# Decay rows by a broadcast DMA instead of matmuls, and parts of the gates and of head 4 in another order

## The chip, the cores and the metric

One core of a Trainium2 chip runs the whole program. The metric is the device time of one execution in microseconds (us). One more execution was taken with a profile; its rows are what is read here.

## What is computed

Two transformer blocks on a sequence of 512 positions with 1024 features, in fp32. The first (stick-breaking attention and a gated FFN) is not touched. The second projects its input, runs two mixers, joins them through two gates, and ends in an MLP. The change lies in the first mixer, branch A, a gated delta rule with 8 heads of 128 query and key features and 256 value features:

```python
qkv = jax.nn.silu(causal_depthwise_conv(jnp.concatenate([qa, ka, va], axis=-1), conv_a))
...
g = -jnp.exp(a_log) * jax.nn.softplus(a_dt + dt_bias)
...
g_cum = jnp.cumsum(g, axis=-1)
decay = jnp.exp(jnp.where(causal, g_cum[..., :, None] - g_cum[..., None, :], -jnp.inf))
lower = jnp.where(strict, jnp.einsum('bhncd,bhnmd->bhncm', k_beta, k) * decay, 0.0)
t_inv = lax.linalg.triangular_solve(lower, eye, left_side=True, lower=True, unit_diagonal=True)
...
attn = jnp.where(causal, jnp.einsum('bhncd,bhnmd->bhncm', q, k) * decay, 0.0)
q_exp = q * jnp.exp(g_cum)[..., None]
def step(state, inp):
    qe, ww, uu, aqk, kd, ld = inp
    v_new = uu - jnp.einsum('bhck,bhkv->bhcv', ww, state)
    o = jnp.einsum('bhck,bhkv->bhcv', qe, state) + jnp.einsum('bhcm,bhmv->bhcv', aqk, v_new)
    state = state * ld[..., None, None] + jnp.einsum('bhck,bhcv->bhkv', kd, v_new)
```

## The kernel before, in words

Every large product is fp32 split in two: a weight half of 128 columns is loaded (`raw`), ScalarE casts it to a high part (`wh`, L122 or L125), VectorE subtracts to get the low part (`wl`, L126), and TensorE does three matmuls for each of 8 slices of the contraction: a unit of 24 matmuls for 128 output features, in one PSUM bank of 512 columns (`psa`, `psg` or `pso`; there are 4, 2 and 2 of them). Two `raw` buffers and four pairs `wh`, `wl` run ahead of TensorE. The loads are issued by SyncE, in the order of the program. All other tiles of branch A live in 32 equal slots (`s`), which go round in the order in which they come free.

Branch A works with chunks of 128 positions, four of them (NT), and two groups of four heads, g0 (heads 0 to 3) and g1 (4 to 7). For each head: `qk_proj` (projection, convolution of 4 taps by L1042 on VectorE, silu by L1046 on ScalarE), `prepare` (norms, scores, decays), and for a group at once `solve` (31 pairs of small steps on VectorE, L1195 and L1198, each waiting for the one before) and `delta_inverse` (joins the blocks that `solve` inverted; its products are masked on POOL by L1225). Then `values_a` (two units, each followed by convolution and silu), `gates_a`, and `delta_scan` (the recurrence over 4 chunks). Projections with no tie to a head (`gate`, `branch_a`) stand between.

`mixer2` writes the order of the large products; the small work is generators that `beside` queues: `yield N` puts the rest of a generator behind N ns of counted TensorE work, `poll` resumes those that are due between matmuls, `until` and `drain` force them. A scheduler then fixes the order of each engine's instructions, and an engine runs them strictly in that order.

The decays: `gates_and_decays` makes g, its sums within a chunk `gc`, and small factors (`ngc` is the negative sum, `kd`, `egl`). `decay_rows` needs for each head the row exp(g_cum) spread over all 128 partitions (`er`), and the masked decay matrix (`dc`, in the program `decT`). Before, TensorE spreads them: four fp32 matmuls of a broadcast g with the triangle `cum` into one bank (`psa<-cst,g`), an exp on ScalarE (L1019) for `er`, four bf16 matmuls that add the mask (`psa<-mb,identb`), and four exps with a bias (L1028) for `dc`.

Of the kernel before, what the change touches and what calls it, by code (L numbers as in the profile page):

```python
# [9 lines left out]
F32 = mybir.dt.float32  # L10
# [60 lines left out]
class Net:  # L71
# [360 lines left out]
    def setup(self):  # L432
# [22 lines left out]
        self.ones = self.const("ones", [P, P])  # L455
        nc.vector.memset(self.ones, 1.0)
# [4 lines left out]
        nc.vector.tensor_scalar(tri[:, 1, :], self.ones, -1.0, None, op0=ALU.mult)  # L461
        nc.vector.tensor_copy(tri[:, 2, :], self.ones)
        self.tri, self.mones, self.pones = tri[:, 0, :], tri[:, 1, :], tri[:, 2, :]
        mb = self.const("mb", [P, 2, P], BF16)

        nc.vector.tensor_scalar(mb[:, 0, :], self.cum, -NEG, NEG, op0=ALU.mult, op1=ALU.add)
        nc.vector.tensor_scalar(mb[:, 1, :], sgn[:, 1, :], NEG, None, op0=ALU.mult)
        self.mask_c, self.mask_s = mb[:, 0, :], mb[:, 1, :]
# [476 lines left out]
    def gates_and_decays(self, acc, heads):  # L945
# [41 lines left out]
        yield 7000  # L987
# [15 lines left out]
        yield from self.decay_rows(heads)  # L1003

    def decay_rows(self, heads):

        nc, S_ = self.nc, self.S
        self.decays = -1
        for h0 in range(heads[0], heads[-1], 2):
            er, dc = self.erow[h0 // 2], self.decT[h0 // 2] = S_.get([P, 2, S]), S_.get([P, 2, S])  # L1010
            ps = []
            for i in range(2):
                p = self.ps("a")
                ps.append(p)
                for n in range(NT):
                    c = slice(n * P, (n + 1) * P)
                    self.mm(p[:, c], self.g[:, n, h0 + i:h0 + i + 1].broadcast_to([P, P]), self.cum,
                            start=(n == 0), stop=False, skip_group_check=True)
                nc.scalar.activation(er[:, i, :], p, AF.Exp)  # L1019
                yield 0  # L1020
            yield 1500
            for i in range(2):
                for n in range(NT):
                    c = slice(n * P, (n + 1) * P)
                    self.mm(ps[i][:, c], self.identb, self.mask_c, start=False, stop=True, skip_group_check=True)
                for n in range(NT):
                    c = slice(n * P, (n + 1) * P)
                    self.last_exp = nc.scalar.activation(dc[:, i, c], ps[i][:, c], AF.Exp,  # L1028
                                                         bias=self.ngc[:, n, h0 + i:h0 + i + 1])
            yield 800  # L1030
# [17 lines left out]
    def first_proj(self, heads):  # L1048

        w = self.a["w_in_2"][0]  # L1050
        r = self.raw(w, 0, KD, O_BE, 16)
# [47 lines left out]
    def prepare(self, h):  # L1099
# [5 lines left out]
        yield 3500  # L1105
# [7 lines left out]
        yield 1600  # L1113
# [421 lines left out]
    def mixer2(self):  # L1535
# [13 lines left out]
        for h in (2, 3):  # L1549
            self.qk_proj(h)  # L1550
# [125 lines left out]
```

## Time and profile before

| what | value |
|---|---|
| median of 3 runs | 2145.35 us (2144.69 to 2147.83) |
| the profiled execution's own time | 2145.01 us |
| its span, first to last instruction | 2142.9 us |
| TensorE (PE) busy | 2079.4 us, 97% |
| VectorE (DVE) busy | 1134.6 us, 53% |
| ScalarE (ACT) busy | 837.8 us, 39% |
| mean granted TensorE clock | 0.994 |
| 680 to 1345 us, branch A up to its last scan: PE busy | 646.9 of 665.0 us |

The profile tells for each engine when it worked and what ended each of its waits. TensorE is busy nearly all the time, so a row matters either when it is TensorE's own work or when TensorE waits for it. Matmuls overlap at their ends: their price is taken from one start to the next, not from the duration of one.

### The profile page before, as it was taken

What the parts mean: (1) busy time and instruction counts of PE and PEld (TensorE: products, weight loads), DVE (VectorE), ACT (ScalarE), POOL (GpSimd) and SP (SyncE); (2) the same over time, 40 slices, a digit from 0 to 9 for tenths busy, and PEclk for the clock granted to TensorE, in tenths of its full rate; (3) what the DMA queues carried; (4) which work ended last, traced back from release to release, by engine and by line L of the source; (5) the groups of instructions that cost most, each with busy time, mean ns of one, the idle gap of its engine ahead of it and who ended that gap; (6) DMA issues with size and microseconds to landing.
All of it is one profiled execution on the core that took longest, in us unless ns stands there. A gap on an engine that the chain in (4) does not pass through costs nothing.

```text
span 2142.9 us, 26115 instructions
## 1 busy us (share of the span) xinstructions
PE 2079.4 (97%) x10498; PEld 1757.2 (82%) x10498; DVE 1134.6 (53%) x1771; ACT 837.8 (39%) x1368; POOL 172.1 (8%) x203
## 2 busy tenths in 40 slices
PE   6899999999999899999998999999999999999998
PEld 5788878888888788888888887888888889888887
DVE  6679778333322565655756545444535475423434
ACT  3587674223212463334522432233232334322422
POOL 2000001000000133000330000010101000000000
PEclk9999999999999999999999999999999999999999
DMA  8715445323232234211342233232222363223322
GB/s 265 211 50 158 142 129 169 117 89 118 89 127 96 103 101 150 78 51 40 125 137 69 83 125 123 84 99 87 77 101 79 139 205 109 98 98 128 98 89 79
DMA packets 172568, 241.93 MB, mean 113 GB/s; under 512 B 13936, under 2 KB 120490, under 8 KB 172448
## 3 DMA queue, kind: packets, MB, share of 16 engines
q1 hardware_dynamic: 168972, 232.65, 33.2%
q0 software_dynamic: 3232, 7.34, 1.5%
q8 instruction: 82, 1.34, 0.3%
q14 instruction: 38, 0.31, 0.0%
q10 hardware_dynamic: 244, 0.29, 0.0%
HBM read 216.59 MB, written 19.41 MB: 110 GB/s over the span
## 4 chain that ended last, share of the span: by engine, by line
PE 84%; DVE 8%; DMA 3%; ACT 2%; issue 1%; POOL 1%; SPq 0%; DVEq 0%; POOLq 0%; ACTq 0%
PE psg L135 37%; PE psa L135 36%; PE pso L135 9%; DMA cv<-ada_w 2%; DVE wl L126 1%; DVE s L1198 1%; PE psa L139 1%; DVE s L1195 1%; DMA s<-ada_w 1%; DVE s L270 1%; DVE s L429 0%; DVE s L501 0%; ACT wh L122 0%; DVE cv L1042 0%; ACT s L291 0%
## 5 line engine op out<-in xcount | busy, mean ns | idle before, releaser
L135 PE MATMUL psg<-s,wh 128*128 128x512 f32 x2368 | 753.5, 398 | 2.5 <-DVE s L1521 2.0
L126 DVE TENSOR_TENSOR wl<-raw,wh 128x1024 fp32r<-128x1024 f32 x306 | 380.9, 1247 | 490.6 <-ACT wh L122 268.8
L135 PEld LDWEIGHTS psg<-s,wh 128*128 128x128 f32 x2368 | 441.1, 189 | 90.7 <-DVE s L1521 2.9
L135 PE MATMUL psa<-wh,s 128*128 128x512 f32 x1536 | 479.1, 391 | 0.3 <-ACT s L272 0.3
L135 PE MATMUL psg<-s,wl 128*128 128x512 f32 x1184 | 464.5, 392 | 0.0
L122 ACT CAST wh<-raw 128x1024 fp32r<-128x1024 f32 x202 | 212.0, 1052 | 436.9 <-PE psg L135 173.7
L135 PEld LDWEIGHTS psa<-wh,s 128*128 128x128 f32 x1536 | 289.4, 189 | 60.3 <-ACT s L272 0.7
L135 PE MATMUL psa<-wl,s 128*128 128x512 f32 x768 | 299.5, 390 | 0.3 <-DVE wl L126 0.3
L135 PEld LDWEIGHTS psg<-s,wl 128*128 128x128 f32 x1184 | 223.2, 189 | 46.7
L135 PE MATMUL psa<-s,s 128*128 128x512 f32 (+3 forms) x760 | 177.4, 364 | 1.0 <-DMA s<-sol 0.6
L135 PEld LDWEIGHTS psa<-wl,s 128*128 128x128 f32 x768 | 144.6, 188 | 30.5 <-DVE wl L126 0.6
L125 ACT CAST wh<-raw 128x1024 fp32r<-128x1024 f32 x104 | 109.1, 1050 | 153.8 <-PE psg L135 122.4
L135 PEld LDWEIGHTS psa<-s,s 128*128 128x128 f32 x760 | 131.1, 190 | 27.4 <-ACT s L1318 2.3
L135 PE MATMUL psg<-wh,s 128*128 128x256 f32 (+1 forms) x672 | 140.9, 298 | 11.0 <-ACT cv L1039 9.2
L135 PE MATMUL pso<-s,wh 128*128 128x512 f32 x448 | 137.9, 389 | 0.0
L135 PEld LDWEIGHTS psg<-wh,s 128*128 128x128 f32 x672 | 110.2, 193 | 16.9 <-ACT cv L1039 9.6
L135 PEld LDWEIGHTS pso<-s,wh 128*128 128x128 f32 x448 | 84.1, 188 | 17.5
L135 PE MATMUL psg<-wl,s 128*128 128x256 f32 (+1 forms) x336 | 97.6, 291 | 0.0
L135 PE MATMUL pso<-s,wl 128*128 128x512 f32 x224 | 87.1, 389 | 0.0
L269 ACT CAST s<-t 128x512 fp32r<-128x512 f32 (+1 forms) x94 | 54.6, 593 | 74.1 <-DVE t L1590 40.6
L270 DVE TENSOR_TENSOR s<-t,s 128x512 fp32r<-128x512 f32 (+1 forms) x94 | 69.2, 747 | 21.3 <-ACT s L269 19.9
L135 PE MATMUL psa<-s,wh 128*128 128x256 f32 x384 | 70.9, 285 | 5.8 <-ACT wh L122 3.1
(244 smaller groups left out, 2199.9 us busy)
## 6 DMA issues: line engine op xcount, KB each, us to landing
raw<-w_in SPq DMA_DIRECT2D x56, 1024.0 KB, 5.2
raw<-ffn_w_in SPq DMA_DIRECT2D x22, 1024.0 KB, 5.1
cv<-ada_w SPq DMA_DIRECT2D x64, 256.0 KB, 4.4
raw<-w_up SPq DMA_DIRECT2D x16, 1024.0 KB, 7.7
raw<-w_down SPq DMA_DIRECT2D x16, 1024.0 KB, 5.1
raw<-sb_w_qkv SPq DMA_DIRECT2D x10, 1024.0 KB
raw<-ffn_w_out SPq DMA_DIRECT2D x10, 1024.0 KB, 6.9
s<-ada_w SPq DMA_DIRECT2D x32, 256.0 KB, 7.3
```

Source lines behind the costliest of these rows:

```text
L122: nc.scalar.copy(h, src)
L125: nc.scalar.copy(h, src)
L126: nc.vector.tensor_sub(l, src, h.bitcast(F32))
L135: self.last_mm = self.nc.tensor.matmul(acc, lhsT, rhs, **kw)
L139: self.last_mm = self.nc.tensor.transpose(out, x, ident)
L269: nc.scalar.copy(dst_h, src)
L270: nc.vector.tensor_sub(dst_l, src, dst_h.bitcast(F32))
L1195: nc.vector.tensor_mul(share, T[:, i, 0:w_].rearrange("p (o j) -> p o j", o=1).broadcast_to([nb, n, w_]), Lb[:, i, i + 1:32].rearrange("p ...
L1198: nc.vector.tensor_add(below, below, share)
```

## The change

Seven edits, all in branch A or in the constants for it.

1. `decay_rows`: the matmuls are gone. `gc` is transposed once for all heads (one PE transpose, one copy on VectorE), written to DRAM (`gcD`, 16 KB), and each head's row is read back by a DMA with a zero step over the 128 partitions (256 KB, pieces of 512 B). VectorE adds bias and mask (four `scalar_tensor_tensor` of 128 x 128 for each head, L1022 of the changed file), ScalarE does two exps of 128 x 512. The function runs at once and no longer as a generator.
2. The constants `mask_c`, `mask_s`, `ones` and `tri` are made a little differently.
3. The delays of `gates_and_decays`, `prepare` and `delta_scan` grow (7000 to 9500, 3500 to 9500, 1600 to 2600).
4. `first_proj` loads its 16 columns into a tile of its own and not into a `raw` buffer.
5. `delta_scan` writes its new values over `vt` and its state over the queries' and keys' slot; it takes two slots less.
6. Two units of gate A go ahead of `qk_proj` of heads 2 and 3.
7. Values and gates of head 4 go ahead of `branch_a(0)`; of the two unit pairs of gate B that stood ahead of `branch_a(0)`, one stays and one goes behind the scans of g1.

```diff
@@ gates_and_decays, decay_rows
-        yield from self.decay_rows(heads)
+        yield 800
+
+        pg = self.ps("a")
+        self.tr(pg[:32, :P], fl(gc), self.ident)
+        rows = self.t2()
+        nc.vector.tensor_copy(rows[:32, :P], pg[:32, :P])
+        self.gcD = self.dp.tile([NT, A_H, P], F32, name="gcD")
+        nc.sync.dma_start(self.gcD.rearrange("n h c -> (n h) c"), rows[:32, :P])
+        self.decay_rows(heads)
...
             for i in range(2):
-                p = self.ps("a")
-                ps.append(p)
+                nc.sync.dma_start(er[:, i, :].rearrange("p (n c) -> p n c", c=P),
+                                  self.gcD[:, h0 + i, :].rearrange("(o n) c -> o n c", o=1).broadcast_to([P, NT, P]))
                 for n in range(NT):
                     c = slice(n * P, (n + 1) * P)
-                    self.mm(p[:, c], self.g[:, n, h0 + i:h0 + i + 1].broadcast_to([P, P]), self.cum,
-                            start=(n == 0), stop=False, skip_group_check=True)
-                nc.scalar.activation(er[:, i, :], p, AF.Exp)
-                yield 0
-            yield 1500
-            for i in range(2):
-                for n in range(NT):
-                    c = slice(n * P, (n + 1) * P)
-                    self.mm(ps[i][:, c], self.identb, self.mask_c, start=False, stop=True, skip_group_check=True)
-                for n in range(NT):
-                    c = slice(n * P, (n + 1) * P)
-                    self.last_exp = nc.scalar.activation(dc[:, i, c], ps[i][:, c], AF.Exp,
-                                                         bias=self.ngc[:, n, h0 + i:h0 + i + 1])
-            yield 800
+                    nc.vector.scalar_tensor_tensor(dc[:, i, c], er[:, i, c], self.ngc[:, n, h0 + i:h0 + i + 1],
+                                                   self.mask_c, op0=ALU.add, op1=ALU.add)
+                nc.scalar.activation(er[:, i, :], er[:, i, :], AF.Exp)
+                self.last_exp = nc.scalar.activation(dc[:, i, :], dc[:, i, :], AF.Exp)
...
@@ first_proj
-        w = self.a["w_in_2"][0]
-        r = self.raw(w, 0, KD, O_BE, 16)
+        nc, w = self.nc, self.a["w_in_2"][0]
+        r = self.t2([P, KD, 16])
+        nc.sync.dma_start(r, w[:, O_BE:O_BE + 16].rearrange("(k p) c -> p k c", p=P))
...
@@ mixer2
+        self.gate(O_GA, "gaD", 0, 2)
         for h in (2, 3):
             self.qk_proj(h)
-        self.gate(O_GA, "gaD", 0, 4)
+        self.gate(O_GA, "gaD", 2, 4)
...
             if h == 4:
-                self.beside(self.decay_rows(g1))
+                self.decay_rows(g1)
                 self.beside(self.prepare_all(g1))
-        self.gate(O_GBT, "gbD", 1, 3)
+        self.gate(O_GBT, "gbD", 1, 2)
+        self.values_a(4)
+        self.gates_a(4)
         self.until(lambda: len(self.oaT) == 8)
         self.branch_a(0)
         for h in g1:
-            self.values_a(h)
-            self.gates_a(h)
+            if h > 4:
+                self.values_a(h)
+                self.gates_a(h)
             self.beside(self.delta_scan(h))
+        self.gate(O_GBT, "gbD", 2, 3)
         self.drain()
```

Three places where instructions stand otherwise now. The names are pool names with running numbers (`s25_263` is slot 25).

The first is TensorE at the decays of g0, right behind the two small matmuls that sum g (`psa_842`). Before:

```order
L135 MATMUL psg_858_6305<-s17_204_5669,wl_857_6302 128x512
L135 MATMUL psa_842_6206<-g_6144,cst_82 128x32
L135 MATMUL psa_842_6206<-g_6144,ones_91 128x32
L135 MATMUL psa_843_6223<-cst_82,g_6144 128x128 x4
L135 MATMUL psa_845_6229<-cst_82,g_6144 128x128 x4
L135 LDWEIGHTS identb_93
L135 MATMUL psa_843_6223<-mb_99,identb_93 128x128
```

Now:

```order
L135 MATMUL psg_852_6272<-s17_204_5668,wl_851_6269 128x512
L135 MATMUL psa_842_6226<-g_6143,cst_82 128x32
L135 MATMUL psa_842_6226<-g_6143,tri_93 128x32
L135 MATMUL psg_852_6272<-s21_205_5669,wh_850_6268 128x512
L135 MATMUL psg_852_6272<-s14_209_5673,wh_850_6268 128x512
L135 MATMUL psg_852_6272<-s21_205_5669,wl_851_6269 128x512
L139 MATMUL psa_854_6279<-cst_82,gc_6229 32x128
L135 MATMUL psg_852_6272<-s21_205_5669,wh_850_6268 128x512
```

The 40 matmuls of the decays have gone from between the units, and one transpose of `gc` (`psa_854`) stands there, three matmuls later. Behind it VectorE now has, where before it had only convolutions and weight splits:

```order
L1007 COPY t_855_6281<-psa_854_6279 32x128
L1037 SCALAR_TENSOR_TENSOR s18_217_5903<-cr_847_6259,convc_107,s18_217_5903 128x510
L126 TENSOR_TENSOR wl_863_6375<-raw_861_6372,wh_862_6374 128x1024
L1037 SCALAR_TENSOR_TENSOR s18_217_5903<-cr_847_6259,convc_107,s18_217_5903 128x509
L126 TENSOR_TENSOR wl_877_6446<-raw_861_6372,wh_876_6445 128x1024
L1022 SCALAR_TENSOR_TENSOR s0_219_6286<-s29_218_6285,ngc_6231,mask_c_99 128x128 x8
L1022 SCALAR_TENSOR_TENSOR s30_221_6302<-s24_220_6301,ngc_6231,mask_c_99 128x128 x8
L1086 TENSOR_REDUCE sm4_867_6398<-t_866_6396 128x4
```

The copy of the transposed rows (L1007) is followed by convolutions and splits, then by the sixteen mask steps (L1022) that read what the DMA brings back; the reduce behind them belongs to `prepare(0)`.

The second is ScalarE in the first scans, at the decays of g1 (L1313 of the changed file is L1318 before: the new values of a scan; L1268 is L1272: gates). Before, between two steps of the scan of head 1:

```order
L1318 ACTIVATE s8_256_7781<-psa_1188_7844,br_1_6557 128x256
L1038 COPY cr_1203_7899<-psg_1187_7840 128x512
L1039 ACTIVATE cv_1202_7898<-psg_1187_7840,convc_108 128x512
L1318 ACTIVATE s8_256_7781<-psa_1194_7867,br_1_6557 128x256
L1046 ACTIVATE cv_1202_7898<-cv_1202_7898 128x512
L1340 ACTIVATE t_1198_7881<-pso_1180_7823 128x512
```

Now, at that scan's first steps:

```order
L1268 ACTIVATE s29_252_7696<-psg_1168_7707 128x256
L1024 ACT_TABLE_LOAD
L1024 ACTIVATE s25_263_8432<-s25_263_8432 128x512
L1313 ACTIVATE s24_246_7501<-psa_1225_7847,br_1_6586 128x256
L1025 ACTIVATE s7_264_8433<-s7_264_8433 128x512
L1024 ACTIVATE s25_263_8432<-s25_263_8432 128x512
L1025 ACTIVATE s7_264_8433<-s7_264_8433 128x512
L1268 ACT_TABLE_LOAD
L1268 ACTIVATE s29_252_7696<-psg_1168_7707 128x256
L1313 ACTIVATE s24_246_7501<-psa_1231_7879,br_1_6586 128x256
```

Four exps of `decay_rows`, whose data come by a DMA through slot 25, now stand between the steps of the scan, and two table loads with them.

The third is VectorE at the end of the second solve (L1195 and L1198, now L1191 and L1194) and the convolution of the values that are projected beside it (L1042, now L1037). Before:

```order
L1198 TENSOR_TENSOR s2_289_9116<-s2_289_9116,s9_290_9119 64x7x25
L126 TENSOR_TENSOR wl_1556_9775<-raw_1554_9772,wh_1555_9774 128x1024
L1195 TENSOR_TENSOR s9_290_9119<-s2_289_9116,s22_279_8624 64x156
L1042 SCALAR_TENSOR_TENSOR cv_1508_9486<-cr_1509_9487,convc_108,cv_1508_9486 128x511
L1198 TENSOR_TENSOR s2_289_9116<-s2_289_9116,s9_290_9119 64x6x26
L1042 SCALAR_TENSOR_TENSOR cv_1508_9486<-cr_1509_9487,convc_108,cv_1508_9486 128x510
L1195 TENSOR_TENSOR s9_290_9119<-s2_289_9116,s22_279_8624 64x135
L1042 SCALAR_TENSOR_TENSOR cv_1508_9486<-cr_1509_9487,convc_108,cv_1508_9486 128x509
```

Now:

```order
L1194 TENSOR_TENSOR s22_282_9232<-s22_282_9232,s20_283_9235 64x2x30
L1191 TENSOR_TENSOR s20_283_9235<-s22_282_9232,s13_269_8532 64x31
L1194 TENSOR_TENSOR s22_282_9232<-s22_282_9232,s20_283_9235 64x31
L126 TENSOR_TENSOR wl_1619_9816<-raw_1617_9813,wh_1618_9815 128x1024
L1037 SCALAR_TENSOR_TENSOR cv_1548_9559<-cr_1549_9560,convc_107,cv_1548_9559 128x511
L1037 SCALAR_TENSOR_TENSOR cv_1548_9559<-cr_1549_9560,convc_107,cv_1548_9559 128x510
L1037 SCALAR_TENSOR_TENSOR cv_1548_9559<-cr_1549_9560,convc_107,cv_1548_9559 128x509
L126 TENSOR_TENSOR wl_1696_9999<-raw_1617_9813,wh_1695_9998 128x1024
```

The convolution that stood between the solve's last steps was of head 4's first unit; the one that now follows the whole solve is of head 5's first unit, and head 4's stand far ahead of it.

## Rows read from the trace of the kernel before

**Rows 1.** The page, part 4: the chain that ended last, by engine.

```profile
PE 84%; DVE 8%; DMA 3%; ACT 2%; issue 1%; POOL 1%; SPq 0%; DVEq 0%; POOLq 0%; ACTq 0%
```

**Rows 2.** Waits of PE: us, times, longest.

```profile
PE psg L135 <- ACT cv L1039: 9.2, 2, 8.0
...
PE psa L135 <- ACT wh L122: 3.1, 2, 2.7
```

**Rows 3.** Timeline of PE at the decays of heads 0 to 3: start, us.

```profile
753.58 2.03 PE L135 MATMUL psa<-cst,g 128*128 128x128 f32 x16
...
757.83 0.71 PE L135 MATMUL psg<-s,wh 128*128 128x512 f32 x2
```

**Rows 4.** Timeline of PE at the decays of heads 4 to 7.

```profile
1005.42 1.05 PE L135 MATMUL psa<-cst,g 128*128 128x128 f32 x8
1006.23 0.71 PE L135 MATMUL psg<-s,wh 128*128 128x512 f32 x2
...
1009.97 0.62 PE L135 MATMUL psa<-mb,identb 128*128 128x128 bf16 x8
1010.40 0.70 PE L135 MATMUL psg<-s,wh 128*128 128x512 f32 x2
```

**Rows 5.** Timeline of ACT behind the first unit of head 4's values.

```profile
1138.79 0.63 ACT L1046 ACTIVATE cv<-cv 128x512 f32<-128x512 f32 x1 [11.71 <-DVE cv L1042]
```

**Rows 6.** Timeline of DVE during the second solve.

```profile
1099.98 0.17 DVE L1195 TENSOR_TENSOR s<-s,s 64x31 f32<-64x31 f32 x1
...
1115.57 0.41 DVE L1195 TENSOR_TENSOR s<-s,s 64x255 f32<-64x255 f32 x1
...
1118.59 1.40 DVE L1195 TENSOR_TENSOR s<-s,s 64x256 f32<-64x256 f32 x1
...
1136.20 0.73 DVE L1042 SCALAR_TENSOR_TENSOR cv<-cr,convc,cv 128x511 f32<-128x511 f32 x1
```

**Rows 7.** Timeline of POOL during the second solve.

```profile
1123.46 5.75 POOL L1225 TENSOR_TENSOR s<-s,cst 128x512 f32<-128x512 f32 x4
```

**Rows 8.** Timeline of PE at values and gates of head 4.

```profile
1141.48 0.58 PE L135 MATMUL psg<-wh,s 128*128 128x256 f32 x1 [8.03 <-ACT cv L1039]
```

**Rows 9.** Windows: PE busy, PEld, DVE, ACT, POOL, granted clock, DMA share, GB/s.

```profile
1138.50:1145.30 6.80, 3.82 (x18) 3.82 (x19) 5.29 (x14) 3.54 (x6) 0.00 (x0) 0.50 0.36 101
1145.30:1152.10 6.80, 6.80 (x55) 6.55 (x55) 0.00 (x0) 1.49 (x3) 0.00 (x0) 1.00 0.36 109
1288.50:1292.20 3.70, 3.70 (x9) 2.63 (x10) 1.34 (x3) 0.91 (x2) 0.00 (x0) 0.54 0.23 71
1292.20:1296.00 3.80, 3.80 (x17) 2.94 (x17) 3.77 (x6) 1.66 (x2) 0.00 (x0) 1.00 0.00 0
```

**Rows 10.** Timeline of SP ahead of branch A.

```profile
719.19 0.38 SPq L111 DMA_DIRECT2D raw<-w_in  x1
```

**Rows 11.** Timeline of PE at the end of the last scan.

```profile
1286.15 1.94 PE L139 MATMUL psa<-cst,s 128*128 128x128 f32 x8 [1.11 <-DVE s L1353]
```

**Rows 12.** Timeline of SP at the first solve's results.

```profile
880.00 0.51 SPq L1200 DMA_DIRECT2D sol<-s  x1
...
884.16 6.16 SPq L1220 DMA_DIRECT2D s<-sol  x10
```

**Rows 13.** All DMA issues of the trace: KB each, median us to landing.

```profile
raw<-w_in SPq DMA_DIRECT2D x56, 1024.0 KB, 5.2
...
cv<-ada_w SPq DMA_DIRECT2D x64, 256.0 KB, 4.4
...
s<-norm_g SPq DMA_DIRECT2D x3, 512.0 KB, 4.4
```

**Rows 14.** Groups of DVE by form: busy us, mean ns of one.

```profile
L1161 DVE SCALAR_TENSOR_TENSOR s<-psa,sm,s 128x128 f32<-128x128 f32 x32 | 11.0, 344 | 2.7 <-PE psa L135 2.7
```

**Rows 15.** Groups of ACT: busy us, mean ns of one.

```profile
L1019 ACT ACTIVATE s<-psa 128x512 f32<-128x512 f32 x8 | 4.6, 614 | 1.2 <-PE psa L135 1.1
...
L1046 ACT ACT_TABLE_LOAD x2 | 2.6, 1283 | 0.0
```

More of the change, by code (lines that the diff above doesn't have):

```diff
@@ L454, in setup @@
         nc.vector.memset(self.phalf, 0.5)
-        self.ones = self.const("ones", [P, P])
-        nc.vector.memset(self.ones, 1.0)
         self.identb = self.const("identb", [P, P], BF16)
@@ L460, in setup @@
         nc.vector.tensor_copy(tri[:, 0, :], sgn[:, 0, :])
-        nc.vector.tensor_scalar(tri[:, 1, :], self.ones, -1.0, None, op0=ALU.mult)
-        nc.vector.tensor_copy(tri[:, 2, :], self.ones)
+        nc.vector.memset(tri[:, 1, :].bitcast(F32), -1.0)
+        nc.vector.memset(tri[:, 2, :].bitcast(F32), 1.0)
         self.tri, self.mones, self.pones = tri[:, 0, :], tri[:, 1, :], tri[:, 2, :]
[L464 to L468, printed above, removed]
+        self.ones = self.pones.bitcast(F32)
+        self.mask_s = self.const("mask_s", [P, P], BF16)
+        nc.vector.tensor_scalar(self.mask_s, sgn[:, 1, :], NEG, None, op0=ALU.mult)
+        self.mask_c = self.const("mask_c", [P, P])
+        nc.vector.tensor_scalar(self.mask_c, self.cum, -NEG, NEG, op0=ALU.mult, op1=ALU.add)
         pt = self.ps("a")
@@ L986, in gates_and_decays @@
         self.g = g
-        yield 7000
+        yield 9500
         pc = self.ps("a")
@@ L1104, in prepare @@
         g0 = h // 4 * 4
-        yield 3500
+        yield 9500
         if h == g0:
@@ L1112, in prepare @@
             self.silu(t[:, i, :])
-        yield 1600
+        yield 2600
         q, kk = t[:, 0, :], t[:, 1, :]
@@ L1296, in delta_scan @@
         st = None
-        vs, ss = (S_.get([P, 4, A_DV]) for _ in range(2))
         pos = []
@@ L1316, in delta_scan @@
             self.mm(pv, Y[:, cs], R, start=True, stop=True)
-            vn = vs[:, n, :]
+            vn = vt[:, n, :]
             nc.scalar.activation(vn, pv, AF.Copy, scale=self.brk[h][:, n:n + 1])
@@ L1322, in delta_scan @@
                 self.mm(pu, kdec[:, cs], vn, start=True, stop=True)
-                s2 = ss[:, n, :]
+                s2 = self.qk[h][:, :, cs]
+                pu = pu.rearrange("p (i c) -> p i c", i=2)
                 if n > 0:
@@ L1333, in delta_scan @@
         self.scanned = h
-        S_.put(vt, vs, ss, self.qk[h], self.ka[h])
+        S_.put(vt, self.qk[h], self.ka[h])
         if h % 2 == 1:
@@ L1354, in delta_scan @@
                                            op0=ALU.mult, op1=ALU.mult)
-        yield 7000
+        yield 9500
         for j in range(2):
```

2 lines of the change are left out of this document (removed).

## Prediction

> **What bounds it now.** The chain of work that ended last comes first: 84% of it is TensorE, 8% VectorE, 3% DMA [rows 1]. So a matmul that goes is a gain, and a wait counts only where TensorE stands in it. The list of TensorE's waits comes next. In the part that the change touches it has two entries: 9.2 us, of which 8.0 at once, for L1039, the evacuation of a values unit, and 3.1 us for L122, the cast of a weight [rows 2]. Third, the timelines around these waits say what is behind them.
>
> The long wait: in front of the gates of head 4 TensorE stands 8.03 us until 1141.48, so from 1133.45 on [rows 8]. ScalarE could not evacuate the unit, because the silu ahead of it stood 11.71 us until 1138.79 behind the convolution [rows 5]; it had been free since 1127.08. The convolution started only at 1136.20, since VectorE's order put it behind nearly all steps of the solve, which began at 1099.98 [rows 6]. When TensorE came back its granted clock was 0.50, the lower of its two levels, for 6.8 us; 18 matmuls took 3.82 us there, and in the next 6.8 us, at 1.00, 55 matmuls took 6.80 [rows 9].
>
> **The change, part by part.**
>
> *Decay matmuls gone.* From start to start: for g0 753.58 to 757.83, 4.25 us [rows 3], and one later piece of eight mask matmuls, 0.43. For g1 there are four pieces of eight fp32 records, of which one shows 0.81 (1005.42 to 1006.23; the four are 0.81, 0.81, 0.88 and 0.90), and two mask pieces of 0.43 (1009.97 to 1010.40) [rows 4]. Sum 4.68 + 4.26 = 8.9 us. One new transpose takes at most the mean of eight at the lower clock, 1.94 / 8 = 0.2 [rows 11]. Term: **-8.7**. Nothing else of TensorE's work changes in amount.
>
> *Values of head 4 ahead of branch A.* In the changed order VectorE takes the whole solve of g1 before the convolution of head 5's first unit, and head 4's convolutions stand ahead of the solve. From the solve's start to the end of that unit TensorE has six units of 24 matmuls; at 3.80 / 17 = 0.224 us for one [rows 9] that is 32 us. Before it had 27 (1099.98 to 1127.08). The solve took 36.2 us up to the convolution [rows 6]. Eight of its steps took 1.40 where their like took 0.41, while POOL multiplied (5.75 us for four) [rows 6, 7]; without these it would be 28. Before, the convolution could have started 1.1 us after the evacuation without a wait: it started at 1136.20, TensorE at 1141.48, 5.3 us later, and the wait began at 1133.45. So now the wait is 0 if the solve is done in 28 us, and about 36.2 + 1.2 for a weight split - 33 - 1.1 = 3.3 if POOL disturbs it as much as before. POOL's products need slots that the branch gives back late, so it meets the solve's end alone: I take 1.0. Term: 8.0 to 1.0, **-7.0**. The low clock behind it cost 3.82 - 18 x 6.80 / 55 = 1.6: **-1.6**.
>
> *Gate B behind the scans.* At the end of the last scan TensorE waits 1.11 us, runs eight transposes in 1.94 [rows 11], and nine matmuls in 3.70 at a granted 0.54, which are 9 x 0.224 = 2.0 later [rows 9]. Two units, 10.7 us of work that waits for nothing, now lie there. Term 1.1 + 1.7 and a little for the transposes: **-3.0** (bounds 0 and -4).
>
> *Small weight out of the raw buffer.* The load of the second 1 MB went out at 719.19, when the small one was split [rows 10], and TensorE waited 3.1 us for its cast [rows 2]. Now both large loads can go out ahead. The small load in turn is issued behind SyncE's stores of x, but TensorE needs it after 23 matmuls of 256 columns instead of 12. **-2.5** (bounds 0 and -3.1).
>
> *Decays by DMA, g0.* This is the new wait. Times on the old time axis: the transpose stands three matmuls behind 753.58, so 754.3; the copy comes behind one convolution step (0.73 as in [rows 6]), 755.6. No row shows a store of 16 KB and its reads. The nearest is the solve's store and its first read, 880.00 to 884.16, 4.2 us [rows 12]: reads go out at 759.9. Four reads of 256 KB are 1 MB: at the least one such load, 4.4, at the most four one after the other, 17.6; I take that of a 1 MB load, 5.2 [rows 13], which is the same bytes on the same queue, and the last lands at 765.1. Of 16 mask steps at 0.34 [rows 14] the second eight begin there at the earliest: 768.0. The last two exps, 0.61 each, a table load of 1.28 [rows 15] and two silus of 0.63 [rows 5] follow: 771.7. In the changed order TensorE comes to the transposes of these queries 63 matmuls of 0.224 and some 0.5 behind 754.3, at 768.9. It waits 3, and then a little for a PSUM bank behind the same silus: **+3.5** (bounds 0 and 16).
>
> The Trainium skill, in "DMA: Bandwidth & Descriptors" (Anatomy of one DMA), gives a DMA about 2 us fixed and its bytes at 436 GB/s on top. An estimate by that page would put store and reads at 2.0 + 4.4 = 6.4 us in place of the 9.4 above, the wait at 0.5, and the whole at 2125.5. The trace's own pair of store and read took longer than the page has it, and the rows are what I go by.
>
> *Decays by DMA, g1.* The slots of the scans of heads 0 and 1 receive the rows. The read can only go out when a scan has left its slot, and in the order ScalarE's exps stand ahead of the next new values of the scan. For the first pair TensorE has some 36 matmuls of 256 columns and six small ones between, 36 x 0.124 + 0.8 = 5.2; the chain needs 0.5 + 4.4 (a 256 KB load) + 4 x 0.34 + 0.61 + 0.4 = 7.3: 2 us late. The second pair has about 6 us and is late by 0 to 1. Term **+2.5** (bounds 0 and 10). The longer row of VectorE (32 steps, 11 us) and three more table loads, 3.8 us, are hidden, since both engines are idle about half the time; uncovered, at such a place, they are in the chains above. Delays, constants and the shared slots are nothing by themselves: their instructions take the same forms. The smaller wait for L1039 (9.2 - 8.0 = 1.2) I leave.
>
> **Sum:** -8.7 - 7.0 - 1.6 - 3.0 - 2.5 + 3.5 + 2.5 = -16.8. From the profiled execution's own 2145.0 that is 2128.2; the median is 0.35 above it: **2128.5 us**.
>
> **Rivals.**
>
> *The new waits don't show* (0.16). Reads land as fast as 256 KB do, and nothing is left of the wait at the values: another 3.5 + 2.5 + 1.0 off, 2121.5. For it: DMA is little used. Against: the chain of g0 has seven links.
>
> *The old wait comes back one head later* (0.20). If VectorE begins the solve some 5 us later, or POOL meets all of it, the convolution of head 5 is as late as head 4's was; 7.0 + 1.6 return: 2137.1. For it: VectorE's order has the whole solve ahead of that convolution, where before some steps came behind it.
> The Trainium skill's "GPSIMD Engine Reference" (Key points) says that GpSimd shares its SBUF interfaces with VectorE and contends with instructions of two SBUF inputs; by this, every step of the solve, and the new mask steps, are exposed. The trace agrees for the solve's steps, 1.40 against 0.41 [rows 6].
>
> *The reads are served one after another* (0.07; this one ends slower). Broadcast loads of 512 KB took 4.4 [rows 13], so a zero step alone is no brake; but these have pieces of 512 B. If each of the four takes 4.4 behind the one before, g0's last lands 12.4 us later, and each pair of g1 4 later; VectorE, ScalarE and TensorE stand in order behind them: 2128.5 + 12.4 + 8 = 2148.9. From 21.1 us of additional waiting on it is slower by over 0.2%: from 4.6 us for one read.
>
> *Half of these*, no change to speak of (0.07): some old waits remain and some reads are late, 2141 to 2149.6.
>
> **Numbers.** My own forecast has 0.46, with 2124 to 2134 as its range; below 2117 I put 0.04. From 2117 to 2141 lie the forecast and the first two rivals, 0.82. About 0.2%, 4.3 us, is what a measurement of this kernel can tell from no change: faster 0.86, within 0.07, slower 0.07.
>
> **What would show it.** No `psa<-cst,g` group in the trace and TensorE's busy time less by about 9 us; the wait for the evacuation of values down from 9.2 to 1 to 3 us, and no stretch at 0.50 clock near it; none at the end of the scans; new waits of TensorE for the silu or the evacuation of gate A at g0 (about 3.5 us) and for the new values of a scan at g1 (about 2.5); the cast wait at the start below 1 us. I am wrong if the sum of the new waits is over 12 us, if the reads take over 8 us to land, or if a values unit waits again as long as before.

## The result, and the profile after

Four runs of the changed kernel have a median of 2130.99 us (2130.32 to 2131.68), against 2145.77 before: a ratio of 0.993, with a 95% interval of 0.9913 to 0.9947. It is 14.8 us faster; 2128.5 were forecast. The total came out within 2.5 us. Its parts did not, and the experiments show that one of them is the other way round. All medians here are of fast runs: one run of e1_masks_dve (2295.86 us) and one of e8_both (6692.44 us) ended slow and are left out.

The page of the changed kernel, part 1 and part 4:

```profile
PE 2067.2 (97%) x10403; PEld 1749.0 (82%) x10403; DVE 1141.7 (54%) x1803; ACT 836.6 (39%) x1347; POOL 171.9 (8%) x203
...
PE 85%; DVE 6%; DMA 4%; ACT 2%; issue 1%; POOL 1%; SPq 0%; DVEq 0%; POOLq 0%; ACTq 0%
```

TensorE is busy for 2067.2 us where it was 2079.4: 12.2 of the 14.1 us that the span lost are busy time (work at the low clock counts in it with its full length), and 1.9 are waits. So the sum of all waits has hardly changed, though the large ones of branch A have moved. The list of TensorE's waits, the two longest entries that lie in branch A:

```profile
PE psg L135 <- ACT cv L1034: 6.3, 1, 6.3
...
PE psa L139 <- ACT s L1041: 4.2, 1, 4.2
```

The first answers to the 9.2 us of [rows 2]: it is now 6.3 at once (8.0 before), for the same evacuation (L1039 before, L1034 now). The second is new: transposes that wait for a silu.

**The first group's decays.** Timelines of SyncE, VectorE, ScalarE and TensorE in turn (start in us, duration, and in brackets how long the engine stood before it and for whom):

```profile
752.79 0.33 SPq L1009 DMA_DIRECT2D gcD<-t  x1
755.56 2.02 SPq L1018 DMA_DIRECT2D s<-gcD  x4
```

```profile
752.49 0.27 DVE L1007 COPY t<-psa 32x128 f32<-32x128 f32 x1
...
760.81 3.24 DVE L1022 SCALAR_TENSOR_TENSOR s<-s,ngc,mask_c 128x128 f32<-128x128 f32 x12 [2.90 <-DMA s<-gcD]
765.87 1.14 DVE L1022 SCALAR_TENSOR_TENSOR s<-s,ngc,mask_c 128x128 f32<-128x128 f32 x4 [1.82 <-DMA s<-gcD]
```

```profile
767.58 0.61 ACT L1025 ACTIVATE s<-s 128x512 f32<-128x512 f32 x1
768.20 1.28 ACT L1041 ACT_TABLE_LOAD   x1
769.49 1.15 ACT L1041 ACTIVATE s<-s 128x512 f32<-128x512 f32 x2
```

```profile
770.17 1.52 PE L139 MATMUL psa<-cst,s 128*128 128x128 f32 x8 [4.21 <-ACT s L1041]
```

The rows follow the chain link by link: the copy at 752.49, the store at 752.79, the reads from 755.56 on, the first mask steps at 760.81 after VectorE had stood 2.90 us for them, the last four at 765.87 after another 1.82, then the exps, the table load, the silus, and TensorE's transposes at 770.17, 4.21 us late. The reads are what is slow. The group of DMA issues:

```profile
s<-gcD SPq DMA_DIRECT2D x8, 256.0 KB, 8.8
```

That is 8.8 us to landing in the median, for 256 KB. From the first issue at 755.56 until the last four mask steps could begin, at 765.87, the four reads of the first group took 10.3 us, where I had put 5.2, the landing of one 1 MB load, for all four [rows 13].

**The first scans.** TensorE there, at the second group's decays:

```profile
933.72 0.70 PE L135 MATMUL pso<-s,s 128*128 128x256 f32 x2 [0.47 <-DVE s L1350]
...
935.10 0.70 PE L135 MATMUL psa<-s 128*128 128x256 f32 x2 [0.45 <-DVE s L1325]
...
953.65 0.70 PE L135 MATMUL pso<-s,s 128*128 128x256 f32 x2 [0.39 <-DVE s L1350]
```

These are three waits, 1.3 us together, all for VectorE and none for ScalarE's new values (L1313).

**The values.** VectorE, POOL and TensorE at the end of the second solve:

```profile
1099.12 0.17 DVE L1191 TENSOR_TENSOR s<-s,s 64x31 f32<-64x31 f32 x1
...
1103.38 1.23 DVE L126 TENSOR_TENSOR wl<-raw,wh 128x1024 fp32r<-128x1024 f32 x1 [3.06 <-ACT wh L125]
...
1121.81 1.48 DVE L1191 TENSOR_TENSOR s<-s,s 64x231 f32<-64x231 f32 x1
...
1134.18 2.32 DVE L126 TENSOR_TENSOR wl<-raw,wh 128x1024 fp32r<-128x1024 f32 x1
1136.42 5.12 DVE L1037 SCALAR_TENSOR_TENSOR cv<-cr,convc,cv 128x511 f32<-128x511 f32 x3
```

```profile
1134.12 3.53 POOL L1221 TENSOR_TENSOR s<-s,cst 128x512 f32<-128x512 f32 x2 [5.97 <-DVE s L1191]
...
1138.08 2.92 POOL L1221 TENSOR_TENSOR s<-s,cst 128x512 f32<-128x512 f32 x2
```

```profile
1144.33 0.58 PE L135 MATMUL psg<-wh,s 128*128 128x256 f32 x1 [6.34 <-ACT cv L1034]
```

The wait is there again, one head later. The solve begins at 1099.12 and is done just before 1134.18. On the way VectorE stands 3.06 us for a weight's cast that comes before its next step in the order (before, it stood 3.38 at the same place), and four steps take 1.0 us longer (one of them is the 1.48 at 1121.81). Then, while POOL multiplies from 1134.12 to 1141, one weight split takes 2.32 us (1.23 at 1103.38) and the three convolution steps 5.12 (0.73 each in [rows 6]).

**The low clock.** In branch A it stands in two places, behind the two waits:

```profile
771.80:773.50 1.70, 1.70 (x5) 1.31 (x5) 1.46 (x4) 1.70 (x3) 0.89 (x1) 0.50 0.79 299
1144.10:1149.20 5.10, 4.87 (x23) 4.87 (x24) 4.83 (x8) 1.08 (x3) 0.00 (x0) 0.50 0.72 214
```

Columns as in [rows 9]: the granted clock is 0.50, the lower of its two levels, in both windows. The stretch of low clock at the end of the scans has gone.

**The start.** The three waits that are left there are 0.74, 0.84 and 0.62 us, all for the input's transposed halves, and none for a weight's cast any more:

```profile
715.23 0.38 PE L135 MATMUL psa<-s,wh 128*128 128x256 f32 x1 [0.74 <-ACT s L269]
716.46 0.39 PE L135 MATMUL psa<-s,wh 128*128 128x256 f32 x1 [0.84 <-DVE s L270]
...
718.41 0.39 PE L135 MATMUL psa<-s,wh 128*128 128x256 f32 x1 [0.62 <-DVE s L270]
```

Before, they were 0.8, 1.9 and the 3.1 us of [rows 2]: 3.6 us are saved.

### The profile page after: what moved, and what is told of

The parts are those of the page before. It is cut to its first block, busy times and chain, and to the rows that moved or that the text cites. A ratio compares the mean times of both kernels' runs of the same rounds, so it can differ in the third digit from the quotient of the medians.

```text
span 2128.8 us, 25960 instructions
## 1 busy us (share of the span) xinstructions
PE 2067.2 (97%) x10403; PEld 1749.0 (82%) x10403; DVE 1141.7 (54%) x1803; ACT 836.6 (39%) x1347; POOL 171.9 (8%) x203
## 4 chain that ended last, share of the span: by engine, by line
PE 85%; DVE 6%; DMA 4%; ACT 2%; issue 1%; POOL 1%; SPq 0%; DVEq 0%; POOLq 0%; ACTq 0%
PE psg L135 38%; PE psa L135 36%; PE pso L135 9%; DMA cv<-ada_w 2%; PE psa L139 1%; DVE wl L126 1%; DMA s<-gcD 1%; DMA s<-ada_w 1%; DVE s L270 0%; DVE s L500 0%; PE pso L322 0%; DVE s L1194 0%; DMA raw<-w_out 0%; DVE s L1191 0%; PE pso L1493 0%
## 5 line engine op out<-in xcount | busy, mean ns | idle before, releaser
L135 PE MATMUL psa<-s,s 128*128 128x512 f32 (+3 forms) x712 | 161.8, 360 | 0.8 <-DMA s<-s 0.7
L135 PEld LDWEIGHTS psa<-s,s 128*128 128x128 f32 x712 | 123.0, 190 | 21.5 <-issue 1.5
L135 PEld LDWEIGHTS psg<-wh,s 128*128 128x128 f32 x672 | 111.3, 194 | 14.1 <-ACT cv L1034 6.5
L135 PEld LDWEIGHTS pso<-s,wh 128*128 128x128 f32 x448 | 84.1, 188 | 17.6
L425 POOL TENSOR_TENSOR sm<-sm,mhalf 128x1 f32<-128x1 f32 x16 | 10.1, 631 | 807.2 <-DVE sm L423 807.2
```

What stands on the lines that cost most here:

```text
L135: self.last_mm = self.nc.tensor.matmul(acc, lhsT, rhs, **kw)
L425: nc.gpsimd.tensor_tensor(out=r, in0=m, in1=self.mhalf[:, :1], op=ALU.pow)
```

## The experiments

Each was run four or more times, one of them with a profile, against the kernel before on the same chip; before had medians of 2144.1 to 2145.7 us there. Not all experiments ran on one chip, so differences among the changed kernels are in part between chips. The start of branch A differs by up to 4 us between profiled executions of kernels that are equal up to there, so a difference of a few us between two medians can be chance from ahead of the edit. The last column leaves that part out: it is the stretch, in the one profiled execution, from the start of branch A's first wait to the end of TensorE's 1.0 us wait at the last projection of the second mixer (L1518 of the changed file). Behind that point all these traces have the same 621.5 to 622.3 us.

| label | what differs | median us | ratio to before, interval | stretch us |
|---|---|---|---|---|
| before | | 2145.77 | | 807.2 |
| after | the change | 2130.99 | 0.993 (0.9913 to 0.9947) | 792.4 |
| e1_masks_dve | second group's mask products on VectorE | 2119.77 | 0.989 (0.9873 to 0.9906) | 782.8 |
| e2_filler_mid | gate B pair ahead of head 5's values | 2133.63 | 0.9947 (0.9926 to 0.9967) | 796.7 |
| e3_prep_late | prepare of head 0 later | 2121.75 | 0.9896 (0.9874 to 0.9917) | 788.6 |
| e4_decay_mm | the change with decays by matmuls | 2131.1 | 0.9937 (0.9922 to 0.9952) | 795.4 |
| e5_before_dma | before, with decays by DMA | 2152.54 | 1.0043 (1.0027 to 1.0059) | 818.7 |
| e6_vals4_back | head 4's values behind branch A again | 2124.08 | 0.9908 (0.9893 to 0.9924) | 788.3 |
| e8_both | e1 and e3 | 2114.16 | 0.9866 (0.9842 to 0.9891) | 779.9 |
| e9_split | e8, mask steps and exps later than the reads | 2116.92 | 0.9877 (0.9858 to 0.9897) | 780.4 |
| e10_rows2k | the change, rows of 2 KB | 2123.49 | 0.9906 (0.9891 to 0.9921) | 786.6 |
| e11_bdelays | before, with the longer delays | 2144.48 | 1.0001 (0.9991 to 1.001) | 809.0 |
| e12_both_mm | e8 with decays by matmuls | 2127.63 | 0.9924 (0.9907 to 0.9941) | 791.7 |
| e13_all | e8 with rows of 2 KB | 2113.95 | 0.9863 (0.9848 to 0.9877) | 777.2 |

### What the wait at the values is made of: e1 and e2

e1_masks_dve:

```diff
-                nc.gpsimd.tensor_mul(C[:, i, :].rearrange("p (n c) -> p n c", c=P), LT,
+                (nc.vector if g0 else nc.gpsimd).tensor_mul(C[:, i, :].rearrange("p (n c) -> p n c", c=P), LT,
```

> The changed kernel, but the eight mask products of the second group's inversion (L1221) run on VectorE in place of POOL. In the changed kernel's trace TensorE waits 6.3 us for the evacuation of head 5's first values unit, behind a convolution that VectorE reaches at 1136.4 and that takes 5.1 us. Theory, contention with POOL: while POOL multiplies, five steps of the solve take 1.0 us longer each, a weight split 1.1 and the three convolution steps 2.9, together 9 us; without POOL there VectorE gains 9, pays about 0.7 for each of the six products that now lie ahead of the convolution's end (4.2), and the wait falls from 6.3 to about 1.6, the low clock behind it (2.3 us lost) goes with it: 2124 to 2126 us. Rival, the order alone: the convolution is late because the whole solve stands ahead of it, VectorE's own products make up for what POOL cost, the wait stays at 5 to 7 us and the time at 2130 to 2132.

Measured: 2119.77, below the theory's 2124 to 2126: 11.2 us faster than the change, and 9.6 in the stretch. VectorE, three rows around the convolution, and TensorE at the same place:

```profile
1130.14 0.74 DVE L1037 SCALAR_TENSOR_TENSOR cv<-cr,convc,cv 128x511 f32<-128x511 f32 x1
...
1131.67 0.68 DVE L1221 TENSOR_TENSOR s<-s,cst 128x512 f32<-128x512 f32 x1
1132.28 0.74 DVE L1037 SCALAR_TENSOR_TENSOR cv<-cr,convc,cv 128x509 f32<-128x509 f32 x1
```

```profile
1135.80 0.39 PE L135 MATMUL psg<-wh,s 128*128 128x256 f32 x1 [0.46 <-ACT cv L1034]
```

The convolution steps take 0.74 again and a product costs VectorE 0.68; TensorE waits 0.46 us in place of 6.3, less than the theory's 1.6, and no low clock follows. So the wait was made by POOL's products beside VectorE (they slowed four steps of the solve, not five as I had counted). That the solve stands ahead of the convolution would not have been enough: here too all of it but its last two steps, of 0.2 us each, does.

e2_filler_mid:

```diff
         self.branch_a(0)
+        self.gate(O_GBT, "gbD", 2, 3)
         for h in g1:
...
-        self.gate(O_GBT, "gbD", 2, 3)
         self.drain()
```

> The changed kernel, but the last unit pair of gate B stands between branch A's first half and the values of head 5, not behind the scans. Theory, TensorE only comes too early: it arrives 10.7 us later at head 5's values, the wait of 6.3 us and the 2.3 us of low clock behind it go, and what the pair hid at the end of the scans comes back, about 3.3 us: 2125 to 2127. Rival, VectorE is behind for good: the inversion's products or the next convolutions wait in its place, and the time is 2130 to 2135.

Measured: 2133.63. The rival holds. TensorE's waits in branch A:

```profile
PE psa L135 <- ACT t L1232: 4.0, 1, 4.0
PE psa L139 <- ACT s L1041: 3.9, 1, 3.9
PE psa L139 <- DVE s L1350: 2.5, 1, 2.5
```

The wait for the evacuation of values has gone, as the theory had it; in its place the products of the inversion wait 4.0 us, and the end of the scans 2.5. The second row is the first group's, as in the change. The pair behind the scans is worth having: without it that end waits again, and the granted clock falls to 0.50 there (1277.16 to 1280.57).

### What the decays by DMA are worth: e4, e5 and e12

e4_decay_mm puts back the four fp32 and four bf16 matmuls for each head and their exps, with the generator and the mask constants that they need; all other edits stay:

```diff
-        self.decay_rows(heads)
+        yield from self.decay_rows(heads)
...
-                nc.sync.dma_start(er[:, i, :].rearrange("p (n c) -> p n c", c=P),
...
+                    self.mm(p[:, c], self.g[:, n, h0 + i:h0 + i + 1].broadcast_to([P, P]), self.cum,
+                            start=(n == 0), stop=False, skip_group_check=True)
```

> The changed kernel, but with the decays by matmuls as before (all other edits stay). Theory, the ledger of the two traces: 8.9 us of TensorE work come back, and the waits that the DMA made go (4.2 at the first group, some 1.7 of low clock, 1.3 in the first scans): slower by 1 to 3 us, 2132 to 2134. Rival, the decays by DMA are worth all of their matmuls and the waits at these places have other causes: slower by 8 to 9, 2139 to 2140.

Measured: 2131.1, the same as the change; in the stretch it is 3.0 us longer, which the theory had (1 to 3). So the edit that takes the matmuls away brings 0 to 3 us in this kernel. Where the rest goes, by the page of the profile and by the waits of this run:

```profile
PE 2075.0 (98%) x10498; PEld 1755.2 (82%) x10498; DVE 1132.1 (53%) x1770; ACT 838.9 (39%) x1369; POOL 173.4 (8%) x203
```

```profile
PE psg L135 <- ACT cv L1038: 4.0, 1, 4.0
...
PE pso L135 <- DVE s L1354: 1.6, 2, 0.8
```

With the matmuls TensorE is busy 2075.0 - 2067.2 = 7.8 us longer, and its wait at the values is 4.0 in place of 6.3; the wait of 4.2 at the first group is not there. In the first scans 0.8 us are left (the first of the two waits for L1354) of the change's 1.3, so not all of that 1.3 is the reads' doing. The waits that came with the reads took back most of what the matmuls cost.

e5_before_dma is the other corner: the kernel before, with `decay_rows`, `gcD` and the constants of the change and nothing else of it. Against before:

```diff
-                self.beside(self.decay_rows(g1))
+                self.decay_rows(g1)
...
+        self.gcD = self.dp.tile([NT, A_H, P], F32, name="gcD")
+        nc.sync.dma_start(self.gcD.rearrange("n h c -> (n h) c"), rows[:32, :P])
```

> The kernel before with the decays by DMA alone (and the constants, for space); delays and order as before. Theory, what the matmuls save is lost again in waits for the rows: 8.9 us off, 4 to 6 back at the first group and 1 to 3 in the first scans, the wait at head 4's values as before: 2141 to 2145. Rival, the gain of the whole change is this edit: 2135 to 2138.

Measured: 2152.54, 8.4 us slower than before on that chip (2144.1), which neither side had. TensorE's waits:

```profile
PE psa L135 <- DMA s<-sol: 11.7, 2, 6.1
...
PE psa L139 <- ACT s L1040: 4.6, 2, 3.1
...
PE psg L135 <- DVE wl L126: 2.3, 1, 2.3
```

The products of both inversions now wait for the solve's results from DRAM, 11.7 us in two waits (before, 0.6 us at this line), beside 4.6 for silus and 2.3 for a weight split. The theory was right that the gain is lost in waits, and short by two of them. So in the order and with the delays of before, decays by DMA push work behind them over its time; which of the other edits mends this in the change was not tried.

e12_both_mm is e8_both (below), where the waits at the values and most of those at the first group are covered, with the matmuls of e4.

> As e8_both, but with the decays by matmuls. Theory, the 8.9 us of matmuls count once the waits around them are covered, less the 2.7 and 0.6 us that the reads still cost there: 5 to 7 above e8_both's 2115.5, 2120 to 2123. Rival, the decays by DMA bring nothing here either, as in e4_decay_mm: 2114 to 2117.

Measured: 2127.63, above what either side had, against 2114.16 for e8_both and 2113.95 for e13_all. So where their waits are covered the decays by DMA are worth 13.5 us and more by the medians, and 11.8 and 14.5 in the stretch, more than the 8.9 that I had priced for the matmuls. The pages of the profile say the same of TensorE's busy time, here e12_both_mm's and, with the DMA, e13_all's:

```profile
PE 2076.0 (98%) x10498; PEld 1756.2 (83%) x10498; DVE 1131.7 (53%) x1778; ACT 838.3 (39%) x1369; POOL 162.1 (8%) x195
```

```profile
PE 2063.7 (98%) x10403; PEld 1746.9 (83%) x10403; DVE 1136.8 (54%) x1812; ACT 839.4 (40%) x1349; POOL 158.9 (8%) x195
```

12.3 us of busy time go with 96 matmul records and one transpose more. 8.5 of these are the removed matmuls themselves, from start to start; the other 3 to 4 us are spread over the matmuls around them, and what makes them longer there I have not settled.

### Where the time of head 4's values went: e6 and e11

e6_vals4_back:

```diff
         self.gate(O_GBT, "gbD", 1, 2)
-        self.values_a(4)
-        self.gates_a(4)
         self.until(lambda: len(self.oaT) == 8)
         self.branch_a(0)
         for h in g1:
-            if h > 4:
-                self.values_a(h)
-                self.gates_a(h)
+            self.values_a(h)
+            self.gates_a(h)
```

> The changed kernel, but values and gates of head 4 stand behind branch A's first half again (the pair of gate B stays behind the scans). Theory, the edit only moves the wait from head 4's values to head 5's: 2129 to 2133. Rival, as predicted for it, the edit is worth about 7 us and more with the clock: 2137 to 2140.

Measured: 2124.08. Neither: without this edit the kernel is 6.9 us faster, and 4.1 in the stretch.

```profile
PE psa L139 <- ACT s L1041: 3.4, 1, 3.4
PE psg L135 <- ACT cv L1034: 2.2, 1, 2.2
```

The wait for the evacuation of values is 2.2 us here, where it was 8.0 before and is 6.3 in the change. By VectorE's order the convolutions of head 4 stand in the first half of the second solve in this kernel. The solve runs from 1093.01 to 1135.6; its first step and the first convolution step:

```profile
1093.01 1.29 DVE L1191 TENSOR_TENSOR s<-s,s 64x31 f32<-64x31 f32 x1
...
1107.86 0.74 DVE L1037 SCALAR_TENSOR_TENSOR cv<-cr,convc,cv 128x511 f32<-128x511 f32 x1
```

The move of head 4's values, for which I had put down the largest gain, is a loss.

e11_bdelays, the longer delays alone on the kernel before, asked whether they bring this about. (The step from 1600 to 2600 is the second one of `prepare`, and `delta_scan` goes from 7000 to 9500; the list of edits puts this otherwise.)

```diff
-        yield 7000
+        yield 9500
...
-        yield 3500
+        yield 9500
```

> The kernel before with the longer delays alone (gates_and_decays 7000 to 9500, prepare 3500 to 9500 and 1600 to 2600, delta_scan 7000 to 9500). Theory, much of the gain that is not the decays' comes from here: in VectorE's order the convolutions of head 4 now stand in the first third of the second solve and not at its end, and the wait of 8.0 us and the low clock behind it shrink to 2 to 3 us: 2136 to 2140. Rival, the delays only give the reads time and do nothing by themselves: 2143 to 2147.

Measured: 2144.48, no change. My theory falls: the wait at the values is 6.2 us there, though the convolutions stand in the middle of the solve there and not at its end. The delays alone are worth nothing. In e4 and e6 they stand together with the pair of gate B at the end, the free `raw` buffer, the order of gate A and the shared slots, and these runs don't take that group apart. Undoing the delays in the changed kernel was not tried.

```profile
PE psg L135 <- ACT cv L1039: 6.2, 1, 6.2
```

### The first group's chain: e3, e8, e9, e10 and e13

e3_prep_late:

```diff
-        yield 9500
+        yield 15000 if h == 0 else 9500
```

> The changed kernel, but the first step of prepare for head 0 is due after 15000 and not 9500 ns of TensorE work, so that the transposes behind the decays come one unit later. In the changed kernel TensorE waits 4.2 us there for silus behind the exps, and loses some 1.7 us to the low clock after it. Theory, only the place is wrong: the chain of DMA, mask steps and exps is done when TensorE comes, both go, 2124 to 2126. Rival, the chain is only pushed on: the solve of the first group starts 5.5 us later and a convolution or the inversion waits instead, 2129 to 2133.

Measured: 2121.75, better than the theory's 2124. Of this, about half may be chance: branch A's first wait begins at 710.57 in its profiled execution and at 714.50 in the change's, and the stretch is only 3.8 us shorter. TensorE's waits:

```profile
PE psg L135 <- ACT cv L1034: 3.5, 1, 3.5
PE psg L135 <- ACT s L1377: 2.4, 1, 2.4
```

At the first group 2.4 us are left, now for a PSUM bank: the evacuation of gate A (L1377) stands behind the exps on ScalarE, and the granted clock still falls to 0.50 behind it (768.24 to 771.65). So the theory, by which both would go, holds in part. The wait at the values is 3.5 in place of 6.3, which the theory did not have.

e8_both joins e1 and e3.

> The changed kernel with both mendings that helped alone: the masks of the second group on VectorE, and prepare of head 0 due at 15000 ns. Alone they measured 2121.3 and 2121.8 against 2131.0. Theory, two waits at two places: what is left is the 2.4 us that the second alone still waits for a PSUM bank behind the exps; 2115 to 2119. Rival, both times came from one and the same wait (the second alone also shortened the wait at head 5's values from 6.3 to 3.5 us): 2119.5 to 2122.

Measured: 2114.16, 16.8 below the change. The two alone make 20.5 together; the second alone had part of its gain at the first's place and at the start of branch A. In the stretch they make 9.6 and 3.8 alone and 12.5 together. No wait at the values and no low clock behind the first group is left (the wait for L1377 there is 2.7 us), so these are two waits.

e9_split is e8_both, but `decay_rows` only issues its reads, and mask steps and exps come 12000 ns later (it is a generator again, and prepare of head 0 is due at 20000 ns):

```diff
+        yield 12000
+        for h0 in range(heads[0], heads[-1], 2):
+            er, dc = self.erow[h0 // 2], self.decT[h0 // 2]
             for i in range(2):
                 for n in range(NT):
```

> As e8_both, and decay_rows only issues its reads at first; the mask steps and exps follow 12000 ns of TensorE work later (prepare of head 0 at 20000). Theory, the rows then have landed when VectorE and ScalarE come to them, the 2.4 us at the first group and most of the 1.3 in the first scans go, 2112 to 2115. Rival, the later start of the first solve makes a convolution or the inversion wait: no better than e8_both.

Measured: 2116.92; the interval covers e8_both's. The waits at the first group are gone in its trace, and it brings no time that can be told: its first wait in branch A begins at 713.88, e8_both's at 710.56, and the stretch is 0.5 us longer. Inconclusive.

e10_rows2k asks why the reads take 8.8 us: their pieces of 512 B, or the 1 MB loads beside them on the queue.

```diff
-        self.gcD = self.dp.tile([NT, A_H, P], F32, name="gcD")
-        nc.sync.dma_start(self.gcD.rearrange("n h c -> (n h) c"), rows[:32, :P])
+        self.gcD = self.dp.tile([A_H, S], F32, name="gcD")
+        nc.sync.dma_start(self.gcD.rearrange("h (n c) -> (h n) c", c=P), rows[:32, :P])
...
+                nc.sync.dma_start(er[:, i, :], self.gcD[h0 + i:h0 + i + 1, :].broadcast_to([P, S]))
```

> The changed kernel, but the sums are put in the order of heads before the transpose, so that a head's row lies in one piece of 2 KB in DRAM and not in four of 512 B; the reads are as large as before. In the changed kernel their median to landing is 8.8 us. Theory, the small pieces make them slow: 4 to 5 us to landing, the wait of 4.2 us at the first group falls to 0 to 1.5, 2126 to 2128. Rival, they share their queue with loads of 1 MB, one issued ahead and one right behind: landing stays at 8 to 9 us, the wait at 3.5 to 5, 2130 to 2132.

Measured: 2123.49, below the theory's 2126: 7.5 less than the change, and 5.8 in the stretch.

```profile
s<-gcD SPq DMA_DIRECT2D x8, 256.0 KB, 4.8
```

```profile
PE psg L135 <- ACT cv L1035: 6.3, 1, 6.3
```

The same 256 KB land in 4.8 us. The wait for the silu is no longer in the list, and the wait at the values stands at 6.3 as in the change. The pieces were the cause of the slow landing, and not the neighbours on the queue: the 1 MB loads are issued at 749.87 and 757.95 here, and at 749.93 and 757.95 in the change.

e13_all is e8_both with these rows.

> e8_both with the rows of 2 KB. If small pieces make the reads slow, the 2.7 us at the first group go: 2112 to 2114. If not, as e8_both, 2114 to 2117.

Measured: 2113.95, level with e8_both by the medians and 2.7 us shorter in the stretch: 17.0 us below the change, 1.4% below the kernel before. No wait over 0.9 us is left in branch A.

## Why the prediction was right, and where its steps were wrong

The total was right, through errors that cancel, so the hit is in good part luck. The decays by DMA, -2.7 net in my sum, bring 0 by the medians and 3.0 in the stretch. The move of head 4's values, -8.6, costs 4 to 7. e4_decay_mm, which has the matmuls back, is still 14.6 us below before. So, if these readings add, most of the gain lies in the edits that I had priced at -5.5 together (gate B, the small weight) or at nothing (delays, shared slots, gate A's order). The traces show 3.6 us of it at the start of branch A and the low clock gone at the end of the scans, and e11_bdelays shows that the delays alone bring nothing; what the rest is made of stays open.

Of the signs of being wrong that I had named one came: the reads took over 8 us to land. The new waits make 5.5 us, under 12, and the values unit waited 6.3 us, not 8.0.

**Decay matmuls gone (-8.7).** The group is gone, as said, and the price of its rows was right: 8.5 us from start to start in e12_both_mm. Busy time fell by more, by 12.2 here and by 12.3 between e12_both_mm and e13_all. Not all of the 12.2 is the matmuls' (e4_decay_mm has them all and is busy 4.4 us less than before), but in the second pair 3 to 4 us lay in their neighbours, which a price from the removed rows alone leaves out. In this kernel the term and its waits together bring little (e4_decay_mm: 2131.1).

**Values of head 4 ahead of branch A (-7.0 and -1.6).** Wrong in sign. The second rival came true in kind, "the old wait comes back one head later": 6.3 us in place of the 1.0 that I took, with 5 us of low clock behind it. The step that failed is "POOL's products ... meet the solve's end alone: I take 1.0". Even my bound of 3.3 was short, by three links that it left out. Its 36.2 us reach only to the convolution of before, where 51 of the solve's 62 steps were done; the last eleven take another 3.0 us (1131.21 to 1134.2). The split and the convolution, which come behind the solve, meet POOL as well, at 1.1 and 2.9 us. Against these, POOL slowed four steps of the solve and not eight, 4 us less: 3.3 + 3.0 + 1.1 + 2.9 - 4.0 = 6.3. e1_masks_dve shows POOL to be the cause, and e6_vals4_back that the move costs 6.9 us by the medians. I also held the order of before, with the convolutions late in the solve, for the alternative; with the other edits the alternative is e6's order.

The Trainium skill's "GPSIMD Engine Reference" (Key points) names a mechanism that fits: GpSimd shares SBUF interfaces with VectorE and contends with its instructions of two SBUF inputs. The trace agrees here for solve steps (1.48 us for 0.39), a weight split (2.32 for 1.23) and convolutions (5.12 for three of 0.73).

**Gate B behind the scans (-3.0).** Right in kind: no low clock at the end of the scans, and with the pair elsewhere the wait of 2.5 us is back (e2_filler_mid). Of the wait itself 0.9 us stay (1.1 before).

**Small weight out of the raw buffer (-2.5).** Right, and 3.6 in the waits.

**Decays by DMA, first group (+3.5).** 4.2 us, and then some 1.7 (an estimate: 3.4 us at a granted 0.50, from 770.86 on) for the low clock behind it, which I left out. Two links were mis-sized in opposite directions: store to first read took 2.8 us and not 4.2, and the four reads took 10.3 and not 5.2, within my bounds of 4.4 and 17.6. The copy came 3 us earlier, and so did TensorE. The estimate of 6.4 us for store and reads, worked out from the Trainium skill's "DMA: Bandwidth & Descriptors" (Anatomy of one DMA), was further off than mine: 13.1 were measured (752.79 to 765.87). That section describes DMAs issued by GpSimd; these are issued by SyncE.

**Decays by DMA, first scans (+2.5).** 1.3 us, in three waits of 0.4 to 0.5, and not by the path that I named: none is for the new values behind ScalarE's exps. With the matmuls in their place there are 0.8 us of waits there in e4_decay_mm and 1.5 in e12_both_mm, so at most some 0.5 us of it can be put down to the reads in this kernel.

**The slower rival** did not come true in the change; with the decays by DMA on the kernel before it did (e5_before_dma), by another mechanism than the one I named: the inversion's products wait for the solve's results.

## What to carry to other kernels

Work taken off the engine that bounds a kernel is a gain only as far as what replaces it is ready in time: the same edit lost 8 us, brought 0 to 3 and brought 13.5 in three surroundings, so its own chain wants to be covered first. Before a wait is moved along a fixed order, look at what else runs beside the engine that is late: here a third engine's products made the wait, and moving them was worth more than moving the wait. And where a transfer is on the path, its pieces can matter as much as its bytes: 8.8 us against 4.8 here. Last, a total that comes out right says little about its parts: take each large one out again and measure.

## What the runs showed of the hardware

- A broadcast read of 256 KB from DRAM to 128 partitions, four issued in a row, landed in 8.8 us with pieces of 512 B and in 4.8 with pieces of 2 KB (e10_rows2k; 5.1 in e13_all), beside the same loads.
- While POOL multiplied 128 x 512 tiles, VectorE's fp32 instructions of two SBUF inputs took 1.48 for 0.39 us (64 x 231), 2.32 for 1.23 (128 x 1024) and 1.7 on average for 0.73 (128 x 511).
- The granted clock fell to 0.50 behind waits of 4.2 and 6.3 us in the change; in e1_masks_dve and e6_vals4_back it stayed at 1.00 behind waits of 3.5 and 3.4 us at the first group. In e3_prep_late it fell behind a wait of 2.4 us there, and in e8_both it stayed at 1.00 behind one of 2.7, so the length of the wait alone does not tell.
